# One transformer layer on one core: another fixed order of preparation and attention, the half copies of q on ScalarE, two tiles' convolution sums in PSUM, a gate's split apart from its broadcast

## The chip, the cores and the metric

The kernel runs on one core of one Trainium2 chip. The metric is the time of one execution on the device in microseconds (us). Five engines work side by side: PE (TensorE, matmuls), DVE (VectorE), ACT (ScalarE), POOL (GpSimd) and SP (which issues most of the DMAs). Each runs its own instructions in order and waits for the others through semaphores.

## The reference

One layer of a trunk with attention and a feed-forward part, for 512 latent and 128 context tokens of width 1024; 8 heads of two 64-wide sub-keys, feed-forward width 2816. Cut to what matters here:

```python
h = modulate(x, norm1_w, shift1, scale1)
proj = h @ w_in                                  # u | q | k | v | gates
q = rope_2d(q); k_lat = rope_2d(k)               # latent tokens only
s = einsum(q, concat(ctx_k, k_lat)) * scale      # two maps m = 0, 1 per head
p = softmax(s); a = p[0] - lam * p[1]
o = a @ v                                        # then RMSNorm per head
x += gate1 * ((sig(gA) * (pool(u) @ w_proj_a) + sig(gB) * (o @ w_proj_b)) @ w_out)
h = modulate(x, norm2_w, shift2, scale2)
a, up = split(h @ w_ffn_in)
a = dwconv3(a, ffn_conv_w, ffn_conv_b)           # 3 taps along the tokens
x += gate2 * ((silu(a) * up) @ w_ffn_out)        # then the final RMSNorm
```

with `rope_2d` a product with cos, plus the halves exchanged times sin. The gates, shifts and scales are rows of silu(cond) @ w_ada.

## The kernel before, in words

Tokens lie along the free dimension, channels along the partitions, 128 at a time. Each fp32 operand of a product is split in a high and a low part (`whi`, `wlo` of a weight, `hT[0]`, `hT[1]` of the activations), and each product is three matmuls: hi by hi, hi by lo, lo by hi. ACT casts the high part of a weight, DVE or POOL subtracts for the low part (`wload`, L123 to L127).

The start: norm of x, the rows of the modulation (`ada_...`), h, and the first projections of q0, k0 and q1 are written as short steps, one letter and a number each, and the string `BOOT` (L296 to L300) lists them in the order of the program. `q`, `k` and `w` are a step (six matmuls) of q0, k0 and q1 (`part`).

Attention: the string of `PHASES` (L486 to L495) gives the order, one string for each head. `p` is a projection step of six matmuls (q, k of later heads), `b` the same for v, `Sxy` the scores of token tile x under map y (`attend`: DVE takes the maximum `nm`, ACT the exponential `p` with its sum, for the second map DVE and ACT combine the two), `x` is `between` (the turns `mx` of k), `T` and `P` turn the probabilities of the head before (`pat`, `th`, `tl`) and multiply them by v. Scores share two banks of PSUM.

Ahead of a head's scores stands `rope` (L555): ACT copies the projection out of PSUM to `ry`, DVE shuffles it to `rsh`, POOL multiplies by cos, DVE by sin, DVE adds. `q_part` then makes for each map a cast `qd` (ACT), the low part `ql` (DVE) and a copy of the cast, `t[o]`, in the other 64 partitions (POOL, L584). `k_part` makes `ks` (cast on ACT, low part on DVE). Weights are loaded and split one step ahead of their use (`weights`, L793), q's and k's low part on POOL.

Instructions that are pinned keep the order in which they are written; the others are placed by the scheduler of the compiler.

Feed-forward: 22 tiles of 128 channels, in groups (`cycle`). Tiles 0 and 1 (`i < DIRECT`) form their sum of the convolution, `cv`, in SBUF, later tiles in PSUM (`conv`, `silu`): ACT writes the middle tap with the bias, DVE adds the two others to it, 511 columns for the latent and 127 for the context tokens, ACT applies silu. The second gate `g2` is worked out in steps that hang between the matmuls `acc...` of the output product (`gate2`, called at the places listed in `GATE2`, L1539): its sum is split in `bh_g` (ACT) and `bl_g` (DVE), and `pb_g`, ones times both, spreads it over the partitions (`acc_bcast`).

Of the kernel before, what the change touches and what calls it, by code (L numbers as in the profile page):

```python
# [18 lines left out]
P = 128  # L19
# [48 lines left out]
def trunk_kernel(ctx: ExitStack, tc: tile.TileContext, a: dict, o: list):  # L68
# [205 lines left out]
    def acc_bcast(acc, dst, cols, name):  # L274

        hi, lo = acc_split(acc, name)
        for c in range(2):
            pb = bank1(f"pb_{name}{c}")
            mm(pb, ones, hi[:, c, :], True, False)
            mm(pb, ones, lo[:, c, :], False, True)  # L280
            nc.scalar.copy(dst[c][:, cols], pb)
            if c == 0:
                yield
# [8 lines left out]
    with tc.tile_pool(name="boot", bufs=1, reuse_waits="tile") as boot:  # L292
# [3 lines left out]
        BOOT = ("n0 i0 n1 x0 i1 n2 x1 y0 i2 n3 x2 n4 i3 a00 y1 i4 y2 x3 a01 y3 d10 x4 d11 l10 r0 s0 l11 c0 a10 z0 u0 "  # L296
# [229 lines left out]
    with tc.tile_pool(name="att", bufs=2, reuse_waits="tile") as att:  # L526
# [28 lines left out]
        def rope(ps, name, scale):  # L555

            sh = att.tile([P, TOK], F32, tag="rsh", name=f"rsh_{name}")[:, :LAT]
            y_ = att.tile([P, TOK], F32, tag="ry", name=f"ry_{name}")
            nc.scalar.activation(two(y_), ps[:, :, :HALF], AF.Copy, scale=scale)
            y = y_[:, :LAT]  # L560
            nc.vector.stream_shuffle(sh, y, SHUF)
            nc.gpsimd.tensor_tensor(y, y, cos, ALU.mult)  # L562
            nc.vector.tensor_tensor(sh, sh, sin, ALU.mult)
            nc.vector.tensor_tensor(y, y, sh, ALU.add)
            return y_

        def q_load(h):
            return wcols(w_in, COL_Q + h * P, P, 0, KD, f"q{h}", nc.gpsimd)
# [4 lines left out]
        def q_part(h, ps=None, bank=bankP):  # L573
            if ps is None:
                w = weights("q", h)
                ps = bank(f"psq{h}")
                yield from proj_steps(ps, w, hT)
            y = rope(ps, f"q{h}", 0.125)
            qd = [att.tile([P, TOK], F32R, tag=f"qd{m}", name=f"qd{m}_{h}") for m in range(2)]
            ql = QL[h % 2]  # L580
            for (r, o, t), (_, _, l) in zip(MAPS(qd), MAPS(ql)):
                nc.scalar.copy(t[r], y[r])
                nc.vector.tensor_tensor(l[r], y[r], f(t[r]), ALU.subtract)
                nc.gpsimd.tensor_copy(t[o], f(t[r]))  # L584
            Q[h] = qd, ql
# [39 lines left out]
        def k_part(h, ps=None):  # L625
            if ps is None:
                w = weights("k", h)
                ps = bankP(f"psk{h}")
                yield from proj_steps(ps, w, hT)
            y = rope(ps, f"k{h}", 1.0)  # L630
            k_split(h, y, slice(P, KEYS))
            Y[h] = y
# [160 lines left out]
        def weights(kind, i):  # L793

            n = need.index((kind, i))
            for st in need[n:n + 2]:
                if st not in W:
# [17 lines left out]
        def step(h, op):  # L815
# [9 lines left out]
            elif kind == "P":  # L825
                values(h - 1, i)
            elif kind == "m":
# [289 lines left out]
    def conv(i):  # L1117

        av = AV.pop(i)
        cv = CVS[i] = pools["ffn"].tile([P, TOK], F32, tag="cv", name=f"cv{i}", bufs=3)  # L1120
        w = [vcol[:, V_CW + j * NF + i:V_CW + j * NF + i + 1] for j in range(3)]
        if i < DIRECT:
            SUMS[i] = cv[:, :LAT], cv[:, LAT:]
        else:
            SUMS[i] = PS[i][1], bank1(f"cvp{i}")[:, :PRO]
        segs = tuple(zip(SUMS[i], (av[:, :LAT], av[:, LAT:])))
        for c, x in segs if i >= DIRECT else ((cv, av),):
# [7 lines left out]
    def silu(i):  # L1135
        lat, pro = SUMS.pop(i)
        cv = CVS[i]
        for c, x in ((cv[:, :LAT], lat), (cv[:, LAT:], pro)) if i >= DIRECT else ((cv, cv),):
# [176 lines left out]
    def gate2():  # L1315
        for hf in range(2):
            for acc in ada_acc(ffn, 5 * D, hf, "g2", "s", "yr"):
                yield
            yield from acc_bcast(acc, g2, slice(hf * 512, hf * 512 + 512), f"g2{hf}")
# [219 lines left out]
    GATE2 = ((0, 2), (1, 0), (1, 2), (2, 0), (3, 2), (3, 4), (4, 0), (4, 2), (5, 0), (5, 2), (7, 1), (7, 3))  # L1539
# [55 lines left out]
```

## Time and profile before

| | us |
|---|---|
| median of 3 runs (1078.32 to 1081.81) | 1081.34 |
| the profiled execution | 1082.84 |
| its span, first to last instruction | 1081.1 |
| PE busy | 1038.2 (96%) |
| DVE busy | 822.4 (76%) |
| ACT busy | 549.5 (51%) |
| POOL busy | 317.5 (29%) |

The times are of the device; the profile is of one execution, whose own time stands beside its span. Busy shares are means over stages that differ: the start lasts to about 70 us, attention to about 330, the gates and merged projections to 600, output projection and second norm to 660, feed-forward to the end.

### The profile page before, as it was taken

Reading aid. Unit: us, or ns where it says so; the run is one execution under the profiler, and the core shown is the slowest. Engines: PE = TensorE matmul, PEld = TensorE weight load, DVE = VectorE, ACT = ScalarE, POOL = GpSimd, SP = SyncE. Lnnn points to the kernel's source line nnn. Section 1 sums busy time; section 2 is a strip of 40 time slices with the busy share of each in tenths; the row PEclk is TensorE's granted clock in tenths of the full one; section 3 lists DMA queues with packets and bytes.
Section 4 is the critical chain, followed back from the end, with each engine's and each line's share of the span. In section 5 each row is a group of like instructions: output and inputs, shape, how many; then the busy total and the mean of one; then the engine's idle time right before and its main releaser. Section 6 shows DMA issues by size and latency. Waiting matters only on the chain.

```text
span 1081.1 us, 16773 instructions
## 1 busy us (share of the span) xinstructions
PE 1038.2 (96%) x6559; PEld 970.1 (90%) x6559; DVE 822.4 (76%) x1193; ACT 549.5 (51%) x946; POOL 317.5 (29%) x256
## 2 busy tenths in 40 slices
PE   6997999999999999999999999999999999999997
PEld 4787899989999989999998889999779998899986
DVE  5968988988987678677773568988888874698746
ACT  8636767657676462223242465564345542165524
POOL 4444334243220650000000004462565320354211
PEclk9988999999999999999999999999999999999999
DMA  9840212112111115555555021323443322323312
GB/s 313 231 108 28 67 52 66 41 43 70 42 32 52 57 44 170 160 156 157 156 171 201 1 59 39 99 78 98 136 137 98 97 70 69 98 79 98 118 39 98
DMA packets 128481, 106.11 MB, mean 98 GB/s; under 512 B 4173, under 2 KB 110205, under 8 KB 128402
## 3 DMA queue, kind: packets, MB, share of 16 engines
q1 hardware_dynamic: 126450, 101.93, 31.0%
q0 software_dynamic: 1232, 1.80, 0.8%
q8 instruction: 51, 0.84, 0.3%
q10 hardware_dynamic: 720, 1.31, 0.3%
q14 instruction: 28, 0.23, 0.1%
HBM read 101.36 MB, written 3.67 MB: 97 GB/s over the span
## 4 chain that ended last, share of the span: by engine, by line
PE 66%; DVE 19%; ACT 6%; issue 4%; DMA 2%; POOL 1%; SPq 1%; ACTq 0%; DVEq 0%; POOLq 0%
PE ps_g L157 10%; PE psyb L157 5%; PE psk L157 3%; PE psu L157 3%; PE psya L157 3%; PE pb L157 3%; PE s L157 2%; PE po L157 2%; PE psq L157 2%; DVE nm L688 2%; PE psv L157 2%; PE acc L157 1%; PE pat L160 1%; DVE ks L599 1%; DVE p L698 1%
## 5 line engine op out<-in xcount | busy, mean ns | idle before, releaser
L150 POOL TENSOR_TENSOR s<-raw_fu 128x512 f32<-128x512 f32 x20 | 30.1, 1504 | 299.4 <-DVE spare L150 155.8
L157 PE MATMUL ps_g<-hT,whi_g 128*128 128x320 f32 x512 | 96.7, 311 | 0.0
L157 PEld LDWEIGHTS ps_g<-hT,whi_g 128*128 128x128 f32 x512 | 80.2, 188 | 2.0 <-issue 1.5
L690 ACT ACTIVATE p<-s,nm 128x640 f32<-128x640 f32 (+1 forms) x80 | 56.6, 708 | 40.0 <-DVE nm L688 39.4
L157 PE MATMUL psv<-whi_v,hT 128*128 128x256 f32 x320 | 66.3, 287 | 0.0
L688 DVE TENSOR_REDUCE nm<-s 128x1 f32<-128x640 f32 (+1 forms) x80 | 56.5, 709 | 12.4 <-PE s L157 11.0
L150 DVE TENSOR_TENSOR wlo_f<-s,whi_f 128x1024 fp32r<-128x1024 f32 x40 | 53.1, 1336 | 7.2 <-ACT whi_f L150 6.8
L157 PE MATMUL ps_g<-hT,wlo_g 128*128 128x320 f32 x256 | 58.3, 309 | 0.0
L150 ACT CAST whi_f<-s 128x1024 fp32r<-128x1024 f32 x40 | 42.3, 1058 | 27.0 <-POOL s L150 27.0
L157 PE MATMUL s<-ks,qd 128*128 128x320 f32 x144 | 44.2, 318 | 10.3 <-DVE ks L599 7.1
L157 PEld LDWEIGHTS psv<-whi_v,hT 128*128 128x128 f32 x320 | 53.5, 193 | 0.3 <-ACT whi_v L126 0.3
L150 DVE TENSOR_TENSOR wlo_f<-raw_fa,whi_f 128x1024 fp32r<-128x1024 f32 x22 | 34.5, 1567 | 21.8 <-ACT whi_f L150 21.6
L157 PE MATMUL psyb<-on,whi_pb 128*128 128x320 f32 x256 | 48.1, 310 | 0.0
L157 PE MATMUL psv<-wlo_v,hT 128*128 128x256 f32 x160 | 45.7, 285 | 0.9 <-DVE wlo_v L127 0.9
L157 PE MATMUL s<-ks,ql 128*128 128x320 f32 x144 | 43.0, 308 | 0.0
L157 PEld LDWEIGHTS ps_g<-hT,wlo_g 128*128 128x128 f32 x256 | 42.8, 188 | 0.0
L157 PE MATMUL psk<-hT,whi_k 128*128 128x320 f32 x224 | 42.6, 312 | 0.0
L157 PEld LDWEIGHTS psyb<-on,whi_pb 128*128 128x128 f32 x256 | 40.3, 188 | 0.5
L697 ACT ACTIVATE p<-p,z 128x640 f32<-128x640 f32 (+1 forms) x40 | 29.8, 744 | 20.0 <-DVE z L696 19.8
L157 PEld LDWEIGHTS s<-ks,qd 128*128 128x128 f32 x144 | 27.7, 192 | 12.9 <-POOL ry_q L562 6.8
L698 DVE SCALAR_TENSOR_TENSOR p<-p,z,p 128x640 f32<-128x640 f32 (+1 forms) x40 | 35.0, 878 | 5.4 <-ACT p L697 5.1
L157 PE MATMUL pb<-mg,whi_f 128*128 128x320 f32 x176 | 38.9, 307 | 0.0
(1046 smaller groups left out, 3437.0 us busy)
## 6 DMA issues: line engine op xcount, KB each, us to landing
raw_fa<-in_w_ffn_in_dram SPq DMA_DIRECT2D x22, 512.0 KB, 3.8
raw_fu<-in_w_ffn_in_dram SPq DMA_DIRECT2D x22, 512.0 KB, 4.0
raw_fo<-in_w_ffn_out_dram SPq DMA_DIRECT2D x20, 512.0 KB, 3.6
raw_g<-in_w_in_dram SPq DMA_DIRECT2D x16, 512.0 KB, 4.5
raw_g<-in_w_ada_dram SPq DMA_DIRECT2D x16, 512.0 KB, 3.7
araw_sh<-in_w_ada_dram SPq DMA_DIRECT2D x8, 512.0 KB, 8.4
araw_sc<-in_w_ada_dram SPq DMA_DIRECT2D x8, 512.0 KB, 8.4
raw_v<-in_w_in_dram SPq DMA_DIRECT2D x8, 512.0 KB, 6.2
```

What stands on the lines that cost most here:

```text
L150: pin(getattr(self.eng, op)(*args, **kw))
L157: pin(nc.tensor.matmul(out, s, m, start=start, stop=stop, skip_group_check=more))
L160: pin(nc.tensor.transpose(out, x, ident))
L599: nc.vector.tensor_tensor(t[o, cols], y[r], f(t[r, cols]), ALU.subtract)
L688: nc.vector.tensor_reduce(nm[:, i:i + 1], s, AX.XY, ALU.max, negate=True)
L690: nc.scalar.activation(p.rearrange("p (b n) -> p b n", b=s.shape[1]), s, AF.Exp, bias=nm[:, i:i + 1], accum_out=z[:, i:i + 1])
L697: nc.scalar.activation(p, p, AF.Copy, scale=z[:, 1:2])
L698: nc.vector.scalar_tensor_tensor(A[h, t], A[h, t], z[:, 0:1], p, ALU.mult, ALU.add)
```

## The change

It writes another order in `BOOT` and `PHASES` (the same steps, with one new step `w` in phase 0), takes the cos product of q0, q1 and k0 from POOL to DVE, the half copies of q from POOL to ACT, makes q2's weights ready at the step `w` with DVE and ACT, puts the sums of tiles 0 and 1 in PSUM like the others, and lets a step pass between the split and the broadcast of the second gate. The first string of `PHASES` stands for all.

```diff
-        "3b p 4b 2p 2b S00 S01 2b p S10 2p x p S11 p b S20 2b S21 b S30 3b S31 S40 2b",
-        "3p S00 p S01 2p x 2p T0 S10 4p S11 T1 p P0 p S20 2p S21 P1 T2 2p P2 p S30 p S31 2p S40 2p",
+        "b p b 2p 7b S00 b S01 x w b p S10 2p S11 b p S20 p b S21 4b S30 2b S31 S40 b",
+        "2p S00 2p S01 p x 3p T0 S10 4p S11 T1 p P0 p S20 2p S21 T2 P1 2p P2 p S30 2p S31 p S40 2p",
...
-        def rope(ps, name, scale):
+        def rope(ps, name, scale, eng=nc.gpsimd):
...
-            nc.gpsimd.tensor_tensor(y, y, cos, ALU.mult)
+            eng.tensor_tensor(y, y, cos, ALU.mult)
...
-        def q_load(h):
-            return wcols(w_in, COL_Q + h * P, P, 0, KD, f"q{h}", nc.gpsimd)
+        def q_load(h, *eng):
+            return wcols(w_in, COL_Q + h * P, P, 0, KD, f"q{h}", *(eng or (nc.gpsimd,)))
...
-            y = rope(ps, f"q{h}", 0.125)
+            y = rope(ps, f"q{h}", 0.125, nc.gpsimd if h > 1 else nc.vector)
...
-                nc.gpsimd.tensor_copy(t[o], f(t[r]))
+                nc.scalar.copy(t[o], f(t[r]))
...
-            y = rope(ps, f"k{h}", 1.0)
+            y = rope(ps, f"k{h}", 1.0, nc.gpsimd if h > 0 else nc.vector)
...
-                if st not in W:
+                if st not in W and (st, kind) != (("q", 2), "v"):
...
+            elif kind == "w":
+                W["q", 2] = q_load(2, dve, act)
...
-        if i < DIRECT:
-            SUMS[i] = cv[:, :LAT], cv[:, LAT:]
-        else:
-            SUMS[i] = PS[i][1], bank1(f"cvp{i}")[:, :PRO]
+        SUMS[i] = PS[i][i >= DIRECT], bank1(f"cvp{i}")[:, :PRO]
...
-        for c, x in segs if i >= DIRECT else ((cv, av),):
+        for c, x in segs:
...
-    def acc_bcast(acc, dst, cols, name):
+    def acc_bcast(acc, dst, cols, name, apart=False):
...
         hi, lo = acc_split(acc, name)
+        if apart:
+            yield
...
-            yield from acc_bcast(acc, g2, slice(hf * 512, hf * 512 + 512), f"g2{hf}")
+            yield from acc_bcast(acc, g2, slice(hf * 512, hf * 512 + 512), f"g2{hf}", True)
...
-    GATE2 = ((0, 2), (1, 0), (1, 2), (2, 0), (3, 2), (3, 4), (4, 0), (4, 2), (5, 0), (5, 2), (7, 1), (7, 3))
+    GATE2 = ((0, 2), (1, 0), (1, 2), (2, 0), (3, 1), (3, 2), (3, 4), (4, 0), (4, 2), (5, 0),
+             (5, 2), (7, 0), (7, 2), (7, 3))
```

How it moves instructions shows at three places. The first is DVE behind the split of the second v weight (`wlo_v01`), up to the low parts of the first keys (`ks0_0` and `ks1_0`, the two maps of head 0), ahead of the first scores; before:

```order
L561 STREAM_SHUFFLE rsh_q0_750<-ry_q0_751 128x512
L561 STREAM_SHUFFLE rsh_k0_765<-ry_k0_766 128x512
L563 TENSOR_TENSOR rsh_q0_750<-rsh_q0_750,sin_707 128x512
L563 TENSOR_TENSOR rsh_k0_765<-rsh_k0_765,sin_707 128x512
L564 TENSOR_TENSOR ry_q0_751<-ry_q0_751,rsh_q0_750 128x512
L583 TENSOR_TENSOR ql00_708<-ry_q0_751,qd0_0_757 64x640
L583 TENSOR_TENSOR ql01_709<-ry_q0_751,qd1_0_758 64x640
L564 TENSOR_TENSOR ry_k0_766<-ry_k0_766,rsh_k0_765 128x512
L561 STREAM_SHUFFLE rsh_q1_776<-ry_q1_777 128x512
L563 TENSOR_TENSOR rsh_q1_776<-rsh_q1_776,sin_707 128x512
L599 TENSOR_TENSOR ks0_0_742<-ry_k0_766,ks0_0_742 64x640
L599 TENSOR_TENSOR ks1_0_743<-ry_k0_766,ks1_0_743 64x640
```

and now:

```order
L563 STREAM_SHUFFLE rsh_q0_750<-ry_q0_751 128x512
L563 STREAM_SHUFFLE rsh_k0_765<-ry_k0_766 128x512
L564 TENSOR_TENSOR ry_q0_751<-ry_q0_751,cos_706 128x512
L565 TENSOR_TENSOR rsh_q0_750<-rsh_q0_750,sin_707 128x512
L564 TENSOR_TENSOR ry_k0_766<-ry_k0_766,cos_706 128x512
L565 TENSOR_TENSOR rsh_k0_765<-rsh_k0_765,sin_707 128x512
L566 TENSOR_TENSOR ry_q0_751<-ry_q0_751,rsh_q0_750 128x512
L566 TENSOR_TENSOR ry_k0_766<-ry_k0_766,rsh_k0_765 128x512
L585 TENSOR_TENSOR ql00_708<-ry_q0_751,qd0_0_757 64x640
L585 TENSOR_TENSOR ql01_709<-ry_q0_751,qd1_0_758 64x640
L601 TENSOR_TENSOR ks0_0_742<-ry_k0_766,ks0_0_742 64x640
L601 TENSOR_TENSOR ks1_0_743<-ry_k0_766,ks1_0_743 64x640
```

The cos products of q0 and k0 have joined DVE's row, the add of k0 stands ahead of the low parts `ql`, and the shuffle and sin product of q1 have left the place ahead of the keys. On ACT at the same place, before:

```order
L126 CAST whi_v01_803<-raw_v01_801 128x1024
L559 ACTIVATE ry_q0_751<-psq0_372 128x640
L559 ACTIVATE ry_k0_766<-psk0_361 128x640
L126 CAST whi_q2_809<-raw_q2_807 128x1024
L582 CAST qd0_0_757<-ry_q0_751 64x640
L582 CAST qd1_0_758<-ry_q0_751 64x640
L559 ACTIVATE ry_q1_777<-psq1_429 128x640
L598 CAST ks0_0_742<-ry_k0_766 64x640
L598 CAST ks1_0_743<-ry_k0_766 64x640
```

and now:

```order
L126 CAST whi_v01_803<-raw_v01_801 128x1024
L561 ACTIVATE ry_q0_751<-psq0_394 128x640
L561 ACTIVATE ry_k0_766<-psk0_362 128x640
L584 CAST qd0_0_757<-ry_q0_751 64x640
L584 CAST qd1_0_758<-ry_q0_751 64x640
L600 CAST ks0_0_742<-ry_k0_766 64x640
L600 CAST ks1_0_743<-ry_k0_766 64x640
L586 CAST qd0_0_757<-qd0_0_757 64x640
L586 CAST qd1_0_758<-qd1_0_758 64x640
L561 ACTIVATE ry_q1_777<-psq1_429 128x640
```

The cast of q2's weight (`whi_q2`) has left, the half copies (`qd` from `qd`) stand behind the casts of the keys, and the copy of q1 out of PSUM behind them. The second place is PE where q0's projection (`psq0`) ends, here its last row with what follows up to the key projection of head 1 (`psk1`); before:

```order
L157 MATMUL psq0_372<-hT0_98,wlo_first1_514 128x320 x2
L157 MATMUL psq1_429<-hT0_98,whi_first2_369 128x320 x2
L157 MATMUL psq1_429<-hT1_99,whi_first2_369 128x320 x2
L157 MATMUL psq1_429<-hT0_98,wlo_first2_370 128x320 x2
L157 MATMUL psv00_823<-whi_v01_803,hT0_98 128x256
L157 MATMUL psv00_823<-wlo_v01_804,hT0_98 128x256
L157 MATMUL psv00_823<-whi_v01_803,hT1_99 128x256
L157 MATMUL psv00_823<-whi_v01_803,hT0_98 128x256
L157 MATMUL psv00_823<-wlo_v01_804,hT0_98 128x256
L157 MATMUL psv00_823<-whi_v01_803,hT1_99 128x256
L157 MATMUL psk1_842<-hT0_98,whi_k1_718 128x320 x2
```

and now:

```order
L157 MATMUL psq0_394<-hT0_98,wlo_first1_505 128x320 x2
L157 MATMUL psq1_429<-hT0_98,whi_first2_372 128x320 x2
L157 MATMUL psq1_429<-hT1_99,whi_first2_372 128x320 x2
L157 MATMUL psq1_429<-hT0_98,wlo_first2_373 128x320 x2
L157 MATMUL psq1_429<-hT0_98,whi_first2_372 128x320 x2
L157 MATMUL psq1_429<-hT1_99,whi_first2_372 128x320 x2
L157 MATMUL psq1_429<-hT0_98,wlo_first2_373 128x320 x2
L157 MATMUL psk1_824<-hT0_98,whi_k1_718 128x320 x2
```

The step of q1 (`psq1`) and v (`psv01`) that came ahead now come behind: in both programs 182 rows stand ahead of the first scores. The third place is PE at the second half of the second gate, in the output product (`acc...`); before:

```order
L157 MATMUL acc010C_7950<-wlo_fo016_8073,g00_7016 128x512
L157 MATMUL acc010C_7950<-whi_fo016_8072,g01_7017 128x512
L157 MATMUL pb_g210_8130<-bh_g21_8126,ones_85 128x512
L157 MATMUL pb_g210_8130<-bl_g21_8127,ones_85 128x512
L157 MATMUL acc014_7953<-whi_fo016_8072,g00_7016 128x512
L157 MATMUL acc014_7953<-wlo_fo016_8073,g00_7016 128x512
```

and now:

```order
L157 MATMUL acc010C_7956<-wlo_fo016_8079,g00_7022 128x512
L157 MATMUL acc010C_7956<-whi_fo016_8078,g01_7023 128x512
L157 MATMUL acc014_7959<-whi_fo016_8078,g00_7022 128x512
L157 MATMUL acc014_7959<-wlo_fo016_8079,g00_7022 128x512
L157 MATMUL acc014_7959<-whi_fo016_8078,g01_7023 128x512
L157 MATMUL acc014_7959<-whi_fo016_8078,g00_7022 128x512
L157 MATMUL acc014_7959<-wlo_fo016_8079,g00_7022 128x512
L157 MATMUL acc014_7959<-whi_fo016_8078,g01_7023 128x512
L157 MATMUL pb_g210_8142<-bh_g21_8126,ones_85 128x512
L157 MATMUL pb_g210_8142<-bl_g21_8127,ones_85 128x512
```

The broadcast pair `pb_g` of the gate has moved behind one tile of six matmuls.

## Rows read from the trace of the kernel before

**Rows 1.** The page, part 1: busy us (share), instructions

```profile
PE 1038.2 (96%) x6559; PEld 970.1 (90%) x6559; DVE 822.4 (76%) x1193; ACT 549.5 (51%) x946; POOL 317.5 (29%) x256
```

**Rows 2.** PE's waits: line waited for, total us, times, longest us

```profile
PE s L157 <- DVE ks L599: 7.1, 2, 6.6
...
PE mx L160 <- ACT p L690: 3.3, 3, 1.4
...
PE pb_g L157 <- DVE bl_g L250: 1.9, 2, 1.4
...
PE pf2A L157 <- ACT av L150: 1.4, 1, 1.4
...
PE s L157 <- DVE tl L714: 1.3, 1, 1.3
```

**Rows 3.** Windows: length, busy us by engine, granted clock, DMA share, GB/s

```profile
86.00:91.00 5.00, 4.61 (x21) 4.64 (x22) 4.29 (x8) 2.12 (x5) 0.00 (x0) 0.55 0.00 0
108.00:135.00 27.00, 24.99 (x163) 23.15 (x162) 24.65 (x37) 19.89 (x39) 8.83 (x7) 1.00 0.22 67
```

**Rows 4.** Timeline of PE, 69 to 87 us: start, duration, [idle before]

```profile
69.39 0.46 PE L157 MATMUL psq<-hT,wlo_first 128*128 128x320 f32 x2
...
74.89 0.40 PE L157 MATMUL psv<-whi_v,hT 128*128 128x256 f32 x2
...
75.61 0.40 PE L157 MATMUL psv<-whi_v,hT 128*128 128x256 f32 x2
...
76.45 0.75 PE L157 MATMUL psk<-hT,whi_k 128*128 128x320 f32 x4
...
77.33 0.75 PE L157 MATMUL psk<-hT,whi_k 128*128 128x320 f32 x4
...
86.39 0.61 PE L157 MATMUL s<-ks,qd 128*128 128x320 f32 x1 [6.58 <-DVE ks L599]
```

**Rows 5.** The timeline of the other engines, 69 to 84 us

```profile
69.64 1.05 ACT L126 CAST whi_v<-raw_v 128x1024 fp32r<-128x1024 f32 x1 [0.59 <-issue]
...
70.71 0.70 ACT L559 ACTIVATE ry_q<-psq 128x640 f32<-128x640 f32 x1
70.72 1.23 DVE L127 TENSOR_TENSOR wlo_v<-raw_v,whi_v 128x1024 fp32r<-128x1024 f32 x1 [1.26 <-ACT whi_v L126]
...
71.87 0.74 DVE L561 STREAM_SHUFFLE rsh_q<-ry_q 128x512 f32<-128x512 f32 x1
...
73.93 2.85 POOL L127 TENSOR_TENSOR wlo_q<-raw_q,whi_q 128x1024 fp32r<-128x1024 f32 x1
...
74.45 2.89 DVE L563 TENSOR_TENSOR rsh_k<-rsh_k,sin 128x512 f32<-128x512 f32 x1
...
76.75 1.74 POOL L562 TENSOR_TENSOR ry_k<-ry_k,cos 128x512 f32<-128x512 f32 x1
...
77.26 1.78 DVE L564 TENSOR_TENSOR ry_q<-ry_q,rsh_q 128x512 f32<-128x512 f32 x1
...
83.75 0.69 DVE L563 TENSOR_TENSOR rsh_q<-rsh_q,sin 128x512 f32<-128x512 f32 x1
```

**Rows 6.** The tile qd: ns of one, min/median/max, first and last start

```profile
L582 ACT CAST qd<-ry_q x16: 710/725/732, 79.1 to 293.3; 64x640 fp32r<-64x640 f32 x16
...
L584 POOL CAST qd<-qd x16: 712/1202/1829, 80.0 to 295.3; 64x640 fp32r<-64x640 f32 x16
```

**Rows 7.** The tiles cv and pf2C, DVE's convolution sums

```profile
L150 DVE SCALAR_TENSOR_TENSOR cv<-spare,vcol,cv x8: 338/1526/1789, 662.5 to 679.7; 128x511 f32<-128x511 f32 x4, 128x127 f32<-128x127 f32 x4
...
L150 DVE SCALAR_TENSOR_TENSOR pf2C<-av,vcol,pf2C x2: 754/754/755, 686.0 to 686.8; 128x511 f32<-128x511 f32 x2
```

**Rows 8.** The timeline of DVE and ACT, 675 to 681 us

```profile
675.91 4.13 DVE L150 SCALAR_TENSOR_TENSOR cv<-spare,vcol,cv 128x511 f32<-128x511 f32 x4
...
680.13 0.74 ACT L150 ACTIVATE cv<-cv 128x640 f32<-128x640 f32 x1 [4.41 <-DVE cv L150]
```

**Rows 9.** The timeline of DVE at the gate, 797 us

```profile
797.68 2.19 DVE L250 TENSOR_TENSOR bl_g<-acc_g,bh_g 128x1024 fp32r<-128x1024 f32 x1
```

More of the change, by code (lines that the diff above doesn't have):

```diff
@@ L295, in trunk_kernel @@
         H_POOL = (7,)
-        BOOT = ("n0 i0 n1 x0 i1 n2 x1 y0 i2 n3 x2 n4 i3 a00 y1 i4 y2 x3 a01 y3 d10 x4 d11 l10 r0 s0 l11 c0 a10 z0 u0 "
[4 rows of a table removed]
+        BOOT = ("n0 n1 i0 x0 i1 n2 x1 i2 a00 y0 n4 n3 i3 x2 y2 i4 x3 a01 y3 d10 x4 y1 d11 l10 r0 s0 l11 c0 a10 z0 u0 "
[4 rows of a table added]
         pinned[0] = True
@@ L1119, in conv @@
         av = AV.pop(i)
-        cv = CVS[i] = pools["ffn"].tile([P, TOK], F32, tag="cv", name=f"cv{i}", bufs=3)
+        CVS[i] = pools["ffn"].tile([P, TOK], F32, tag="cv", name=f"cv{i}", bufs=3)
         w = [vcol[:, V_CW + j * NF + i:V_CW + j * NF + i + 1] for j in range(3)]
-        if i < DIRECT:
-            SUMS[i] = cv[:, :LAT], cv[:, LAT:]
-        else:
-            SUMS[i] = PS[i][1], bank1(f"cvp{i}")[:, :PRO]
+        SUMS[i] = PS[i][i >= DIRECT], bank1(f"cvp{i}")[:, :PRO]
         segs = tuple(zip(SUMS[i], (av[:, :LAT], av[:, LAT:])))
-        for c, x in segs if i >= DIRECT else ((cv, av),):
+        for c, x in segs:
             act.activation(c, x, AF.Identity, bias=vcol[:, V_CB + i:V_CB + i + 1], scale=w[1])
@@ L1137, in silu @@
         cv = CVS[i]
-        for c, x in ((cv[:, :LAT], lat), (cv[:, LAT:], pro)) if i >= DIRECT else ((cv, cv),):
+        for c, x in ((cv[:, :LAT], lat), (cv[:, LAT:], pro)):
             act.activation(c, x, AF.Silu)
```

22 rows, old and new, of tables (BOOT, PHASES) are left out of this document.

## The prediction

> **What bounds the kernel now.** I read the page first: PE is busy 1038.2 of 1081.1 us, DVE 822.4, ACT 549.5, POOL 317.5 [rows 1]. PE sets the end, so a change is worth what it takes from PE's waits, from the time PE spends at its lower clock, or from its work; the change removes and adds no matmul. PE stands still for about 43 us. The view of PE's waits says for whom: the one long wait is 6.6 us for the split keys `ks`, then 3.3 us in three waits of the key turns `mx` for exponentials, 1.9 us for `bl_g`, 1.4 us of `pf2A` for the copy `av`, 1.3 us for `tl` [rows 2]. [...]
>
> **The long wait, step by step.** PE starts the first scores at 86.39, after 6.58 us without work [rows 4]. What it waits for starts when q0's projection ends, its last matmuls at 69.39 for 0.46, so 69.85; call it T. The rows behind T [rows 5]: ACT first casts `whi_v`, 1.05, then copies q and k out of PSUM, 0.70 each. DVE splits `wlo_v`, 1.23, and shuffles, 0.74. POOL does the cos product of q, then takes q2's weight split, 2.85, which stands ahead of the cos product of k, 1.74 from 76.75. Meanwhile the sin product of k on DVE takes 2.89 and the add of q 1.78, where the same form takes 0.69 with POOL idle. So the chain is stretched by POOL twice: by its queue and by running beside DVE.
>
> The new order does three things here. (1) Of the same 182 rows of PE that come ahead of the first scores, one step of q1 (six matmuls, 0.88, the distance of the `psk` rows) and one v step (six, 0.72, the distance of the `psv` rows) now come behind q0's end [rows 4]. T moves to 69.85 - 0.88 - 0.72 = 68.25, and PE keeps 2 q1 steps, 3 k1 steps and 8 v steps for the time behind T: 1.76 + 2.64 + 5.76 = 10.16 us. (2) The cos products of q0, q1 and k0 go to DVE, and q2's split leaves its place between them, so POOL has nothing there. (3) The half copies of q go to ACT, behind the casts of `ks`.
>
> The new chain from T, with durations of undisturbed rows [rows 5]: ACT `whi_v` 1.05; DVE `wlo_v` 1.23, to T + 2.3 (q and k are copied out by T + 2.5). Then two shuffles of 0.74 and five ops of 0.69 (cos and sin of q and of k, add of q), 4.9 end to end, some 0.6 less as successive DVE ops start before the former's end: add q is done at T + 6.6 to 7.2. Then five casts on ACT of 0.73 (two of q, two of `ks`, the first half copy) [rows 6], 3.65: the first scores start at T + 10.25 to 10.95 with a handover, 78.5 to 79.2. PE's own cover lasts to 78.4, so a wait of 0.1 to 0.8 stands where 6.6 stood. **Term 1: -7.4 us** (86.39 to 79.0). Ends: -5.9 if a DVE or ACT row of the chain is stretched once as the 2.89 was, -8.7 if the six q0 matmuls that now come earlier also fill an idle stretch ahead of 53 us.
>
> **The rest of phase 0.** In the window at 0.55 PE is 4.61 us busy [rows 3]; at full clock that is 2.5, so 2.1 are won if the low clock does not come back. Against it: the new phase has fewer projection steps between the first scores and the key turn `x`, so `x` and the scores around it wait longer for exponentials, and q2's split now takes 1.23 of DVE and 1.05 of ACT inside the phase. I cost that as one more wait like the longest of `mx`, 1.4 [rows 2], less a little: an estimate. **Term 2: -0.8** (0 to -2.0).
>
> **The rest of attention.** For it: the casts leave POOL, where the 16 took 1.2 us each in the median beside DVE's work; they cost 16 x 0.73 = 11.7 us of ACT instead [rows 6]. Phases 3, 5 and 7 begin with scores at once, so the exponential that `mx` waits for (3.3 us in three waits) starts one to three steps of 0.88 earlier. Against it: ACT has about 26% room in its full stretches [rows 3], and each pair of copies pushes what follows by 1.46. What PE can still win here is bounded by rows 2, some 4.6 us from the `mx` and `tl` rows and a few small waits. **Term 3: -1.0** (-4 to +3): a third of the 3.3 us, the copies paying the rest back.
>
> **Convolution of the first two tiles.** In SBUF the eight DVE ops, four of 511 columns and four of 127, have a median of 1526 ns and go up to 1789; the same op with its sum in PSUM took 754 [rows 7]. So the four ops of conv 1 take DVE at most 3.0 us (if the short ones took as long as the long ones), an estimated 2.2, instead of 4.13 [rows 8], conv 0 the like; ACT pays four more short instructions. Who waits: `silu` of conv 1 ended an idle time of 4.41 on ACT for DVE, `av` was queued behind it, and `pf2A` on PE behind `av`, 1.4 [rows 2, 8]. With `silu` 2 us earlier that wait goes. **Term 4: -1.5** (0 to -2.7, DVE's two relieved stretches helping a later tile too). [...]
>
> **The gate row.** `bl_g` starts at 797.68 and takes 2.19, and PE waits 1.4 for it [rows 2, 9]. Behind it stand six independent matmuls of `acc`, 512 columns wide where those of a `psk` step of 0.88 are 320, so 1.4 us, and the new order puts just these ahead of the broadcast pair. The copy of the gate behind it comes no later than now, since PE reaches it no later. **Term 5: -1.2** (0 to -1.4).
>
> At nothing I cost: the start up to T (the same 143 steps; its waits for `hT` and `araw` may move either way by about 1), the exchanged loads of k3 and the cached keys (both needed a phase later), and the three cos products' 2.1 us on DVE in the boot, covered by PE's 10.16.
>
> **Sum.** -7.4 - 0.8 - 1.0 - 1.5 - 1.2 = -11.9. The profiled execution took 1082.84, 1.74 beyond its span and 1.5 above the median 1081.34: it would come to 1070.9 with a span near 1069.2, and the median to about 1069.4.
>
> **Rivals.**
> *The attention waits close too.* The kernel wins most of term 3's room: PE's `mx` and `tl` waits (4.6) go, and the longer end of terms 1 and 2: 1069.4 - 3.0 - 1.3 - 1.2 = about 1064. For it: POOL's traffic leaves DVE, which was stretched in several rows. Against: DVE is 91% busy there and gets three products and a split more.
> [...]
> *ACT takes POOL's place.* If each pair of half copies delays PE once (exponentials queued behind it hold one of the two score banks), 8 x 1.46 = 11.7 us eat the gain: 1081, no change. If it is met twice for a head, at the exponentials behind it and at the next head's scores, which now come sooner and read the copies, 23.4: 1092.8, slower. It decides from 1.5 us per head on. Against it: ACT's 26% of room is 8.6 us in a head's 33, and the copies are made some steps ahead of their scores.
> *The moved phases do nothing beyond the start*, and terms 3 to 5 fall to zero because another wait ends last at each place: 1081.34 - 8.2 = 1073.
>
> **How the numbers follow.** Chances: the forecast 0.42, with its own range 1066.5 to 1072; the closing waits (below 1066.5) 0.20; the smaller win (the second and the fourth rival, 1072 to 1078) 0.27; ACT without change 0.07; ACT slower 0.04. From 1063 to 1076.5 all but about 2 in 10 is held. No change is within 0.3%, 3.2 us, about what a measurement of this kernel can tell: faster 0.89, same 0.07, slower 0.04.
>
> **What would show it.** Right: the first scores within 1 us of the `psv` step ahead of them, at 78 to 80 us; no stretch with a granted clock of 0.55 behind it; the add of q at 0.7 instead of 1.78; no wait of `pf2A` for `av` and none of `pb_g` over 0.3; ACT's busy time up by about 12 us, POOL's down by some 25. Wrong: a wait of several us for `ks` or `qd` at the first scores; waits of `s` for ACT's `qd` in every head; a new wait in the gate's or FFN's first tiles; or a boot that ends q0 later than 68.5.

## The result and the profile after

The changed kernel takes 1071.78 us (median of 4 runs, 1070.32 to 1072.72) against 1081.05 for the kernel before measured beside it (1078.32 to 1081.81): a ratio of 0.9918, 95% interval 0.9900 to 0.9937, so 8.9 us less (6.8 to 10.8). The forecast was 1069.4. The profiled execution is the fastest of the four, with a span of 1068.5, and the one of before was the slowest of its series (1082.84), so the two spans differ by 12.6 us where the medians differ by 9.3. The stretches below are read from these two profiles and add up to 12.6 us, some 3.7 more than the change is worth; part of that is the clock, as will be seen.

The page of the changed kernel, parts 1 and 2:

```profile
PE 1032.8 (97%) x6559; PEld 965.0 (90%) x6559; DVE 810.9 (76%) x1197; ACT 561.8 (53%) x966; POOL 294.6 (28%) x236
...
PEclk9999999999999999999999999999999999999999
```

ACT has the 12 us more, POOL 23 less that 16 copies, three products and a split make [rows 1]. PE's own busy time fell by 5.4 us with the same 6559 matmuls while the mean granted clock rose from 0.990 to 0.997, by 0.007 of the span or some 7 us: time at a lower clock for the most part, an estimate from these two. Now what PE waits for (line, what, total, times, longest):

```profile
PE pat L160 <- ACT p L692: 3.4, 2, 2.1
...
PE s L157 <- DVE ks L601: 2.3, 2, 1.8
...
PE pf8C L157 <- DVE wlo_f L150: 1.9, 1, 1.9
...
PE s L157 <- ACT p L692: 1.8, 2, 1.2
...
PE pf5A L157 <- ACT av L150: 1.1, 1, 1.1
...
PE mx L160 <- ACT p L692: 0.5, 1, 0.5
```

Against [rows 2]: the 6.6 us for `ks` are gone (the 1.8 left belong to head 1), `mx` fell from 3.3 to 0.5, the waits of `pb_g` for `bl_g` and of `pf2A` for `av` are no longer among the waits; but `pat` and `pf8C`, which waited 1.5 and 0.5 before, wait 3.4 and 1.9. Those two before:

```profile
PE pat L160 <- ACT p L690: 1.5, 1, 1.5
...
PE pf8C L157 <- DVE wlo_f L150: 0.5, 1, 0.5
```

Behind the long wait and up to the end of attention PE's waits sum to 8.6 us before and to 8.5 now: in attention they have moved, not shrunk. The place of the long wait on PE's timeline:

```profile
66.40 0.46 PE L157 MATMUL psq<-hT,wlo_first 128*128 128x320 f32 x2
...
77.45 0.28 PE L157 MATMUL psv<-whi_v,hT 128*128 128x256 f32 x1
77.57 0.31 PE L157 MATMUL s<-ks,qd 128*128 128x320 f32 x1
```

The first scores follow a v step without any idle time, at 77.57 instead of 86.39 [rows 4]. The chain that fed them, on the other engines:

```profile
66.65 1.05 ACT L126 CAST whi_v<-raw_v 128x1024 fp32r<-128x1024 f32 x1 [1.24 <-issue]
...
67.73 1.23 DVE L127 TENSOR_TENSOR wlo_v<-raw_v,whi_v 128x1024 fp32r<-128x1024 f32 x1 [1.94 <-ACT whi_v L126]
...
70.15 0.68 DVE L564 TENSOR_TENSOR ry_q<-ry_q,cos 128x512 f32<-128x512 f32 x1
...
71.95 0.69 DVE L565 TENSOR_TENSOR rsh_k<-rsh_k,sin 128x512 f32<-128x512 f32 x1
72.55 0.68 DVE L566 TENSOR_TENSOR ry_q<-ry_q,rsh_q 128x512 f32<-128x512 f32 x1
...
76.31 1.48 ACT L586 CAST qd<-qd 64x640 fp32r<-64x640 f32 x2
```

The sin product of k, 2.89 in [rows 5], takes 0.69, the add of q 0.68 instead of 1.78, with no work on POOL from 62.8 to 81.2 us. The 0.69 in [rows 5] was not one with POOL idle: POOL's cos product of q1 started 0.11 us behind it, at 83.86, and took 1.70, so not every row beside POOL is stretched. q0's projection ends at 66.86 (the T of the prediction: 66.40 and 0.46), and the first scores stand 10.71 us behind it, where 10.25 to 10.95 was worked out; before it was 16.54. T itself came 3.0 us earlier than before, not 1.6. The windows that answer to [rows 3]:

```profile
86.00:91.00 5.00, 4.91 (x34) 4.47 (x34) 4.53 (x8) 4.90 (x9) 0.29 (x1) 1.00 0.35 105
108.00:135.00 27.00, 26.46 (x178) 25.14 (x177) 23.61 (x41) 20.64 (x38) 4.46 (x4) 1.00 0.19 58
```

No low clock follows, 1.00 where 0.55 stood, and between 108 and 135 us PE is busy for 1.5 us more. In the feed-forward part the convolution sums of tile 0 take 748 to 755 ns in PSUM (answer to [rows 7]), and `bl_g` takes 2.20 as before [rows 9], at 785.26, but its wait has moved:

```profile
L150 DVE SCALAR_TENSOR_TENSOR pf0A<-spare,vcol,pf0A x2: 748/752/755, 651.5 to 652.3; 128x511 f32<-128x511 f32 x2
```

```profile
800.38 0.41 PE L157 MATMUL pf8C<-mg,wlo_f 128*128 128x320 f32 x1 [1.90 <-DVE wlo_f L150]
802.90 0.42 PE L157 MATMUL pf9A<-mg,wlo_f 128*128 128x320 f32 x1 [0.49 <-DVE wlo_f L150]
```

By stretches, from the times at which PE starts the same work in both profiles (the end of attention is the first `psu`, here now and then before):

```profile
307.61 0.75 PE L157 MATMUL psu<-hT,whi_u 128*128 128x320 f32 x4
```

```profile
318.33 0.75 PE L157 MATMUL psu<-hT,whi_u 128*128 128x320 f32 x4
```

The gains and losses: to the first scores 8.8 us won; from there to the first scores of head 1 0.2 lost (24.4 to 24.6); from there to the first `psu`, the end of attention, 2.1 won (207.5 to 205.4); from there to the end 1.9.

### The profile page after: what moved, and what is told of

Same layout as the page of the kernel before. It is cut to its first block, busy times and chain, and to the rows that moved or that the text cites. A ratio compares the mean times of both kernels' runs of the same rounds, so it can differ in the third digit from the quotient of the medians.

```text
span 1068.5 us, 16757 instructions
## 1 busy us (share of the span) xinstructions
PE 1032.8 (97%) x6559; PEld 965.0 (90%) x6559; DVE 810.9 (76%) x1197; ACT 561.8 (53%) x966; POOL 294.6 (28%) x236
## 4 chain that ended last, share of the span: by engine, by line
PE 74%; DVE 12%; ACT 5%; issue 3%; POOL 2%; DMA 2%; SPq 0%; ACTq 0%; POOLq 0%; DVEq 0%
PE ps_g L157 11%; PE psyb L157 5%; PE psk L157 4%; PE psu L157 3%; PE acc L157 3%; PE psya L157 3%; PE pb L157 3%; PE psv L157 3%; PE s L157 2%; PE psq L157 2%; PE po L157 2%; POOL s L150 2%; PE pat L160 1%; DVE nm L690 1%; DMA raw_fu<-in_w_ffn_in_dram 1%
## 5 line engine op out<-in xcount | busy, mean ns | idle before, releaser
L690 DVE TENSOR_REDUCE nm<-s 128x1 f32<-128x640 f32 (+1 forms) x80 | 56.7, 710 | 12.4 <-PE s L157 10.6
L126 ACT CAST whi_g<-raw_g 128x1024 fp32r<-128x1024 f32 x16 | 16.8, 1050 | 40.5 <-PE ps_g L157 21.8
```

The source lines that it names most:

```text
L126: cp.copy(hi[:, :n], rv)
L690: nc.vector.tensor_reduce(nm[:, i:i + 1], s, AX.XY, ALU.max, negate=True)
```

## The experiments

Each kernel was timed against the kernel before on one chip; the ratios compare with 0.9918 for the changed kernel, 0.001 being 1.08 us. The intervals are 1.3 to 3 us wide on either side, that of the changed kernel itself 2, so what is smaller is read from the trace.

**e1, the old start order.** `BOOT` as before, the rest as changed.

> The changed kernel with the old order of the start (BOOT) and all else kept. Theory (the cover behind q0 is what holds PE): q0 ends one q1 step and one v step later, 1.6 us, and only 8.6 us of work lie behind it where the chain of whi_v, rope and splits takes 10.9, so the first scores wait 2 to 2.5 us for ks or qd; time 1073.5 to 1076 against 1071.8. Rival (the order of the start is worth nothing, the gain came from POOL leaving the chain): no wait over 0.5 us at the first scores and a time within 1 us of 1071.8.

Measured: 1070.29, 0.9904 (0.9875 to 0.9932), no slower. The theory falls: the first scores come at 78.37 with no wait. q0's projection ends at 67.50, 2.35 us earlier than before although `BOOT` is the same, and the strings of phase 0 supply the cover; what is left of the order of `BOOT` is another wait, 1.49 us of `psk` for the bank that the copy of k empties, 0.46 in the changed kernel:

```profile
69.87 0.57 PE L157 MATMUL psk<-hT,whi_k 128*128 128x320 f32 x2 [1.49 <-ACT ry_k L561]
```

Up to 76 us the mean granted clock is 0.93 in the three profiles with the old order and 0.96 or 0.98 in those with the new one, whose waits ahead of the first scores are longer instead (14 to 15 us against 13): the two about cancel.

**e2, three cos products back on POOL.**

```diff
-            y = rope(ps, f"q{h}", 0.125, nc.gpsimd if h > 1 else nc.vector)
+            y = rope(ps, f"q{h}", 0.125)
-            y = rope(ps, f"k{h}", 1.0, nc.gpsimd if h > 0 else nc.vector)
+            y = rope(ps, f"k{h}", 1.0)
```

> The changed kernel with the cos products of q0, q1 and k0 back on POOL, q2's weight split left at the step w. Theory (POOL's queue was the price, not the product itself): with nothing ahead of them the two cos products run beside DVE's sin products, the add of k comes 0 to 1 us later, the first scores wait 0 to 1 us, time +0.5 (0 to +1.5). Rival (running beside POOL is the price): a sin product and an add on DVE stretch to 1.4 to 2.9 us each as before, the first scores wait 3 us, time +3.

Measured: 1075.34, 0.9959 (0.9938 to 0.9979), 4.4 us slower than the changed kernel. Each theory has a half. The first scores come at 77.30 after a wait of 0.16, as the first has it; the sin products do stretch, to 1.38 and 1.78, but inside PE's cover. The price is paid behind: q1's chain on DVE now stands ahead of the first maximum `nm`, which starts at 81.02 instead of 78.36, and `mx` waits:

```profile
82.81 0.33 PE L160 MATMUL mx<-ident,ry_k 128*128 128x128 f32 x1 [3.40 <-ACT p L692]
```

All of the price lies in phase 0: from the first scores to those of head 1 it takes 29.1 us, 24.6 in the changed kernel. The scheduler moved 14 rows of DVE with this edit, so the price is not that of POOL alone.

**e3, q2's split back on POOL at the first v step, no step `w`.**

```diff
-                if st not in W and (st, kind) != (("q", 2), "v"):
+                if st not in W:
```

> The changed kernel with q2's weight load and split back at the first v step, low part on POOL, and no step w; the cos products stay on DVE. Theory of the queue: no product of the chain stands behind the split any more, so only one or two DVE rows beside it stretch, 1 to 2 us, the first scores wait about 1 to 1.5 us, and phase 0 gets back 1.2 us of DVE: time 0 to +1. Rival (running beside POOL is the price): 2.4 to 2.9 us of POOL stop DVE for as long, the first scores wait 2.5 us or more and the time is +2.5 to +4 with the low clock behind it.

Measured: 1073.95, 0.9938 (0.9916 to 0.9961). The first scores wait 1.5 us for the half copy of `qd` and attention behind them takes 231.0 us from first scores to `psu` (230.0 in the changed kernel): the queue theory by the trace, its +0 to +1 and the measured +2.2 not told apart.

**e4, the half copies back on POOL.**

```diff
-                nc.scalar.copy(t[o], f(t[r]))
+                nc.gpsimd.tensor_copy(t[o], f(t[r]))
```

> The changed kernel with the 16 half copies of q back on POOL (1.2 us each there) instead of ACT (0.73). Theory: ACT's 11.7 us lie in its idle time and POOL's copies stretch the low parts ql beside them, by 0.3 us each and more, so the time goes up by 1 (0 to +2) and the attention ends 1 us later. Rival (ACT has become a bound in attention, with pat and s waiting 5 us for its exponentials): the copies leave ACT's path and the time falls by 1 to 3 us.

Measured: 1077.44, 0.9976 (0.9960 to 0.9992): 6.3 us slower, three times the most that the theory allowed, and the rival has the wrong sign, with these strings of `PHASES` (e5 and e9 compare the copies with the old ones). From the first scores to `psu` attention takes 236.2 instead of 230.0. DVE's low parts `ql`, in e4 and then in the changed kernel (count, busy us, mean ns):

```profile
L585 DVE TENSOR_TENSOR ql<-ry_q,qd 64x640 fp32r<-64x640 f32 x16 | 16.7, 1045 | 1.1 <-ACT qd L584 0.7
```

```profile
L585 DVE TENSOR_TENSOR ql<-ry_q,qd 64x640 fp32r<-64x640 f32 x16 | 13.1, 817 | 0.6 <-ACT qd L584 0.2
```

That is 3.6 us of DVE in attention, where it is the busiest engine but PE (208.3 of 242 us from 78 to 320, ACT 164.2). PE's waits there grow from 8.5 to 12.7 us, spread over `s`, `mx` and `pat`, and the granted clock, 1.00 all through attention in the changed kernel, is 0.91 from 200 to 220 and from 240 to 260 us. Here too rows moved, more than 20 on DVE.

**e5, the old strings of `PHASES`,** with `w` put behind the `x` of phase 0.

> The changed kernel with the old strings of PHASES (the step w put behind x of phase 0), start, engines, convolution and gate as changed. Theory: between the first scores and the end of attention the new strings are worth about 2 us, so the time is +1 to +3 and the waits of mx for exponentials of phases 1, 3 and 5, 3.3 us in the kernel before, are back. Rival: the strings only move the waits (from mx to pat), time within 0.7 us.

Measured: 1080.71, 1.0008 (0.9994 to 1.0022): as slow as the kernel before, with everything else changed. The first scores stand at 80.46, 5.9 us earlier than before, and `psu` at 317.61 against 318.33: what was won ahead of them is lost behind. That is three times the most that the theory allowed, and the rival fails too. Two thirds of the loss lie in phase 0, which takes 29.5 us from the first scores to those of head 1 instead of 24.6:

```profile
80.46 0.41 PE L157 MATMUL s<-ks,qd 128*128 128x320 f32 x1 [0.28 <-ACT qd L586]
...
110.00 0.30 PE L157 MATMUL s<-ks,qd 128*128 128x320 f32 x1
```

From there to `psu` it is 207.6 against 205.4, the 2 us that the theory had for the strings. PE's waits by total, times and longest:

```profile
PE s L157 <- ACT p L692: 4.9, 5, 1.9
...
PE mx L160 <- ACT p L692: 2.3, 2, 1.5
PE s L157 <- DVE tl L716: 2.0, 1, 2.0
```

**e6, the old gate.**

```diff
-            yield from acc_bcast(acc, g2, slice(hf * 512, hf * 512 + 512), f"g2{hf}", True)
+            yield from acc_bcast(acc, g2, slice(hf * 512, hf * 512 + 512), f"g2{hf}")
```

and the old `GATE2`.

> The changed kernel with the gate's broadcast right behind its split again (old GATE2, no extra step). Theory (the gain is given back at the next wait for DVE): PE waits 1.4 us for bl_g again, but pf8C then waits 0.5 instead of 1.9, since the DVE row that it needs comes at the same time; time within 0.5 us of the changed kernel. Rival (the prediction's term): +1.2 to +1.4.

Measured: 1070.77, 0.9920 (0.9896 to 0.9944), no change. The trace shows the two waits side by side:

```profile
787.73 0.50 PE L157 MATMUL pb_g<-bl_g,ones 128*128 128x512 f32 x1 [1.42 <-DVE bl_g L250]
...
800.62 0.41 PE L157 MATMUL pf8C<-mg,wlo_f 128*128 128x320 f32 x1 [0.54 <-DVE wlo_f L150]
```

1.42 + 0.54 with the old gate, 1.90 with the new one: the row of DVE that `pf8C` needs comes when it came.

**e7, the old convolution** (sums of tiles 0 and 1 in `cv`, as in the diff ahead).

> The changed kernel with the convolution sums of tiles 0 and 1 back in SBUF. Theory: the DVE ops take 1.5 to 1.8 us beside POOL's sums again, silu of tile 1 comes 2 us later, pf2A waits 1.3 us for av; time +1.4. [...]

Measured: 1073.05, 0.9939 (0.9914 to 0.9964), +2.3 with intervals that overlap. By the trace `pf2A` waits 0.93 us for `av` again, and 23.0 us pass from `pf2A` to `pf4A`, 21.9 in the changed kernel. At `pf5A` the changed kernel waits 1.1 us, e7 none and e6, which has the new convolution, none either: that wait comes and goes.

**e8, the split of the third sum earlier,** at the first tile of the second and third group.

```diff
         sums(i, 1)
+        hilo(i, 3)
         hilo(i, 4)
...
-        elif i == first:
-            hilo(i, 3)
```

> The changed kernel with one split brought forward: at the first tile of the second and third group of the feed-forward part the split of the third weight sum stands in the preparation, ahead of the last additions of the group before on DVE, instead of behind the first products. Theory (DVE's queue from bl_g on ends last at pf8C): the wait of 1.9 us of pf8C for wlo_f goes, time -1 to -1.9. Rival (the load of the next tile's weights ends last): pf9A waits instead, time within 0.5 us.

Measured: 1075.52, 0.9960 (0.9946 to 0.9974), 4.5 us slower. The wait of `pf8C` goes, and `pf9A` waits 3.49 where it waited 0.49, with a granted clock of 0.74 from 798 to 811 us. DVE in that stretch:

```profile
797.22 1.79 DVE L1418 TENSOR_TENSOR x<-x,yr 128x512 f32<-128x512 f32 x1
798.93 1.78 DVE L150 TENSOR_TENSOR ul<-raw_fu,uh 128x512 fp32r<-128x512 f32 x1
800.64 0.68 DVE L1417 TENSOR_TENSOR yr<-acc011C,g 128x512 f32<-128x512 f32 x1
801.35 1.05 DVE L1418 TENSOR_TENSOR x<-x,yr 128x512 f32<-128x512 f32 x1
802.33 0.47 DVE L150 TENSOR_TENSOR av<-av,pb 128x320 f32<-128x320 f32 x1
802.73 1.89 DVE L150 TENSOR_TENSOR wlo_f<-raw_fa,whi_f 128x1024 fp32r<-128x1024 f32 x1
```

It works without a pause; another order only chooses who waits for it, and rows put off met POOL's sums, which run from 796.57 on with gaps under 0.1 us (`ul` takes 1.78 us, 0.68 in the changed kernel).

**e9, the start alone.** The kernel before with the new `BOOT`, the three cos products on DVE and q2's split at `w`; old strings, copies on POOL, old convolution and gate.

> The kernel before with the start alone changed: the new BOOT, the cos products of q0, q1 and k0 on DVE, q2's split at a step w behind x of phase 0; old strings of PHASES, half copies on POOL, old convolution and gate. Theory (a package: what PE wins ahead of the first scores is given back in phase 0, where DVE and ACT are the bound): first scores at 78 to 81 us as in the changed kernel, against 86.4 before, but the second head's first scores win 3 us or less; the time is 1 to 4 us under that of the kernel before. Rival (the prediction's sum: each term stands for itself): 8 us under it.

Measured: 1076.41, 0.9968 (0.9955 to 0.9981), 3.5 us under the kernel before. The time is in the range of the theory, its reason is not: the first scores come at 79.49, 6.9 us earlier than before, those of head 1 still 5.5 earlier, where the theory had 3 or less, and `psu` 5.8. So little of what is won ahead of the first scores is given back in this trace. The two spans differ by 6.6 us, the medians by 3.5: the profile of the kernel before is of an execution 2.7 us above the median of its runs beside e9. In phase 0 a wait that the kernel before had as 0.93 is longer:

```profile
79.49 0.38 PE L157 MATMUL s<-ks,qd 128*128 128x320 f32 x1 [0.74 <-DVE ks L599]
89.68 0.63 PE L157 MATMUL s<-ks,qd 128*128 128x320 f32 x1 [2.73 <-ACT p L690]
...
105.26 0.31 PE L157 MATMUL s<-ks,qd 128*128 128x320 f32 x1
...
312.50 0.75 PE L157 MATMUL psu<-hT,whi_u 128*128 128x320 f32 x4
```

e5 has the same start and strings with the copies on ACT, and the new convolution and gate. It is 4.3 us slower than e9, with intervals that do not overlap, and phase 0 takes 29.5 us in it, 25.8 here. So with the old strings the copies on ACT cost time, with the new ones they win it (e4); and with the copies on POOL the new strings win nothing (e4 against e9: 0.9 us slower, with intervals that overlap).

**e10, all but the start:** old `BOOT`, cos and q2's split on POOL, the rest as changed.

> The changed kernel with the old start: old BOOT, all cos products on POOL, q2's split on POOL from the first v step, no step w; new strings of PHASES, half copies on ACT, convolution and gate as changed. Theory (package): the first scores stand at 85 to 87 us after a wait of 5 us or more, and attention behind them takes as long as in the changed kernel or up to 3 us less, since DVE has less to do in phase 0: time +4 to +7 over the changed kernel's 1071.8. Rival (the prediction's sum): +8 or more, the whole of term 1 and 2.

Measured: 1079.28, 0.9989 (0.9973 to 1.0004), 7.7 us slower than the changed kernel and not told apart from the one before; between the bounds of the two expectations. The wait is back, but it is 3.72 us and not 5 or more: q0's projection ends at 67.46, 2.4 us earlier than before, and the first scores stand 14.73 us behind it, 16.54 before. And attention behind them takes 234.9 us, where the expectation had the 230.0 of the changed kernel or less: phase 0 alone takes 28.5, with a granted clock of 0.75 from 82.2 to 89 us and a wait of 2.37 for `mx`.

```profile
82.19 0.42 PE L157 MATMUL s<-ks,qd 128*128 128x320 f32 x1 [3.72 <-DVE ks L601]
```

**e11, projection steps moved to the waits that are left.**

```diff
-        "2p S00 2p S01 p x 3p T0 S10 4p
+        "4p S00 p S01 p x 2p T0 S10 4p
...
-        "S00 4b S01 x 2p T0 2p S10 b p b P0
+        "S00 4b S01 x 3p T0 p S10 b p b P0
-        "S00 p S01 4p x T0 3p S10 P0 S11 p T1 2p S20 3p T2 2p S21 P1 P2 p S30 S31 4p S40 3p",
+        "S00 p S01 4p x 2p T0 2p S10 P0 S11 p T1 2p S20 3p T2 2p S21 P1 P2 p S30 S31 3p S40 3p",
```

> The changed kernel with three strings of PHASES moved by a few projection steps: phase 1 takes two more ahead of its first scores (which wait 1.75 us for ks), phases 4 and 5 one and two more ahead of the first turns T0 (which wait 1.3 and 2.1 us for an exponential). Theory (PE runs ahead of ACT at these places and has work that can stand there): the three waits, 5.1 us, fall under 2 in sum, the time is -1.5 to -4 against the changed kernel. Rival (DVE and ACT are the bound through these phases, so PE waits at the next place instead): waits of attention stay at 8 us in sum, time within 1 us.

Measured: 1081.27, 1.0008 (0.9996 to 1.0020), 9.7 us slower. The three waits fell from 5.1 to 0.8 us, as meant, and others came, 14.3 us in sum: 2.1 of `mx` and 1.4 of `pat` in phases 1 and 2, and the longest where the steps moved had ended a projection sooner and the next one found its PSUM bank not yet emptied by ACT:

```profile
253.84 1.44 PE L157 MATMUL psk<-hT,whi_k 128*128 128x320 f32 x4 [3.46 <-ACT ry_q L561]
```

**e12, all 16 cos products on DVE.**

> The changed kernel with all cos products on DVE, the 13 of the later heads too; all else kept. In the changed kernel these 13 take 1.3 to 1.8 us each on POOL, and the sin products on DVE beside them 1.0 to 1.24 in the mean instead of 0.69. Theory (what POOL reads beside DVE costs DVE as long as it takes, as in the rerun with three products back on POOL): the sin products fall to 0.69, 6 us of DVE come back for 8 us of products, the key and query chains of each head get shorter by about 0.6 us, time -1 to -3. Rival (DVE, 85% busy and more through attention, is the bound, and 13 x 0.6 = 8 us more on it are not paid back): time +1 to +4, the waits of PE in attention rise from 8.5 us.

Measured: 1079.54, 0.9994 (0.9980 to 1.0009), 8.2 us slower. The theory's first half is seen: the sin products of q fall from 1237 to 685 ns in the mean. Its second is not: PE's waits in attention go from 8.5 to 11.9 us, most of them for exponentials:

```profile
PE s L157 <- ACT p L692: 5.2, 5, 2.1
...
PE pat L160 <- ACT p L692: 4.0, 3, 1.6
```

That it is the 8 us of products is not shown: DVE's busy time from the first scores to `psu` is 197.0 us, 198.7 in the changed kernel, so the rows that no longer run beside POOL paid the products back in sum. Nearly 60 other rows of DVE have moved with it, and what remains is where rows stand; which of them costs the time was not told apart.

No version tried beats the changed kernel; e1 and e6 equal it within what can be measured, and e3 and e7 come out 2 us slower with intervals that overlap its own.

## Why the forecast held, and where its steps did not

**Term 1 (-7.4): right, in chain and size; the origin of T was not.** The first scores moved by 8.8 us in the profile: T by 3.0 and the chain behind it by 5.8, forecast 1.6 and about 5.8. Seven profiles with this start (the changed kernel, e4, e6, e7, e8, e11, e12) have the first scores between 76.98 and 80.89, all without a wait, and in each they stand 10.70 or 10.71 us behind the end of q0. What differs is T, 66.27 to 70.18 with a median of 68.5, where 68.25 was forecast; the median of the first scores, 79.2, is 7.2 us earlier than before, so the 8.8 holds some luck of the execution. What POOL costs in the chain shows apart from T: 10.7 us without its products and its split, 11.0 with the cos products back (e2), 12.4 with q2's split back (e3), 14.7 with both (e10). The step that T moves by 1.6 us through the order of the start, and that this supplies the cover, failed in part: with the old `BOOT` and the new strings T is 67.5 (e1, e10), no later than with the new one.

**Term 2 (-0.8): the sign failed.** The low clock behind the wait is gone, 1.00 from 86 to 91 us for 0.55, which I keep at the estimated 2.1 from [rows 3]: before, the score matmuls start 0.27 us apart from 86.79 to 88.39, at a clock of 0.50, and 0.15 apart from 91.81 to 92.25, at 1.00. But the waits from there to head 1's first scores grew from 1.3 us (two of `s` for exponentials) to 3.5 (0.55 of `mx`, 1.21 of `s` for an exponential, 1.75 of head 1's `ks`), by 2.2 and not by the 1.3 that I had allowed: 0.2 lost.

**Term 3 (-1.0): 2.1 in the profile, and costed in the wrong way.** I treated the new strings as something to win a third of `mx`'s waits with and the copies as paying part of that back. e5 and e4 show that the kernel needs both: without the new strings it is 9.7 us slower, without the copies on ACT 6.3. And each needs the other: of the four pairings with the new start, old strings with copies on POOL (e9) or ACT (e5), new strings with copies on POOL (e4) or ACT (the changed kernel), e5 is 4.3 us slower than e9, e4 no faster, and only the last gains, 5.4 us with its convolution.

**Term 4 (-1.5): 1.4 by `pf4A`,** the mechanism as told, by the trace alone, since e7's time does not settle it: sums in PSUM at 0.75 us, no wait of `pf2A` (0.93 in e7). These sums had POOL at work beside them too, two sums of 2.35 and 2.43 us, and were not stretched: 0.75 in PSUM stands against up to 1.79 in SBUF beside POOL. The short sums, 338 ns at the least in SBUF [rows 7], take 348 to 355 in PSUM, some 10 ns more.

```profile
L150 DVE SCALAR_TENSOR_TENSOR cvp<-spare,vcol,cvp x4: 348/353/355, 652.9 to 666.9; 128x127 f32<-128x127 f32 x4
```

A later wait for `av` hides part of it in some executions.

**Term 5 (-1.2): nothing.** The step that failed is "the copy of the gate comes no later, so the wait is won": I followed PE past the pair, not DVE. DVE's queue from `bl_g` on was unaltered: from its start to that of `pf8C` behind its wait 15.1 us pass in both profiles, and PE met it 13 us later at `pf8C`. e6 shows it, and e8 that DVE is full there. One longer wait also stands where two shorter ones stood: in the nine profiles in which `pf8C` waits 1.9 us, the granted clock from 795 to 815 us is 0.91 in five, 1.00 in four; in the three with the old gate (before, e6, e9) it is 1.00. The changed kernel, then e1:

```profile
795.00:815.00 20.00, 17.61 (x119) 17.09 (x119) 18.85 (x21) 9.72 (x16) 13.10 (x8) 1.00 0.28 80
```

```profile
795.00:815.00 20.00, 18.11 (x114) 17.85 (x113) 18.05 (x21) 9.50 (x16) 12.03 (x8) 0.91 0.35 102
```

**The sum.** The terms were added as if each stood for itself. The start alone is worth 3.5 us (e9), all the rest alone 1.2 (e10), both together 8.9: about 4 us, 1 to 7 by the intervals, belong to neither. The traces show where: from the first scores to those of head 1 it takes 24.4 us before and 24.6 in the changed kernel, 25.8 in e9 and 25.9 in e4, but 28.5 in e10, 29.1 in e2 and 29.5 in e5. The three long ones have the half copies on ACT together with the cos products on POOL or the old string of phase 0, and PE's long waits in them are for exponentials of ACT. Why just these pairs cost 4 to 5 us there stays open. I had put DVE's 91% share (24.65 of 27 us [rows 3]) in front of the rival of closing waits only; as a limit on term 1 it was not among the rivals. The forecast of 11.9 less lies 3 us beyond the measured 8.9; that it was no further off owes something to luck, with term 3 half its size in the profile, term 2 of the wrong sign and term 5 nothing.

The rivals: *ACT takes POOL's place* is refuted by e4 for the strings as changed, but with the old ones it holds in part (e5 against e9). A long wait that shrinks and does not go, the second rival of the chances, is what e10 looks like: 3.72 us of it are left, with a granted clock of 0.75 behind it, from 82.2 to 89 us. *The attention waits close too* did not come about, they are 8.5 us. *The moved phases do nothing beyond the start* is refuted by e5 and e9: the start alone wins 3.5 us and not 8.2.

## What to carry to other kernels

Where an engine beside PE is nearly full, as DVE was here with 7.97 of 8 us from 798 to 806, a wait taken away in one place can come back whole at the next one, as 1.4 us did from the gate to `pf8C`: follow the engine that was waited for, not PE, until a place where it has idle time, and only then count the gain. An order written out by hand belongs to the durations it was written for: here each single part put back or pushed on in attention cost 2 to 10 us, so the parts of such a change can't be costed one by one, and alone-and-undone pairs (e9 and e10) measure what they have in common. Which engine should take small copies is a question of that order too: in the new one ACT's 11.6 us (16 of 0.727) were free and POOL's slowed DVE by 3.6 us in `ql`, in the old one the same copies on ACT cost 4.3 us.

## What the runs showed of the hardware

The granted clock is not the same from one execution to the next, behind the same wait. PE waits 2.0 to 2.1 us for an exponential at the second `pat` that waits, in nine of the profiles; from 240 to 262 us the granted clock is 0.92 in six of them and 1.00 in three. The changed kernel and e6 have the same program there:

```profile
240.00:262.00 22.00, 19.56 (x134) 18.36 (x133) 18.63 (x27) 14.50 (x26) 4.44 (x4) 1.00 0.28 81
```

```profile
240.00:262.00 22.00, 19.92 (x129) 19.25 (x128) 18.69 (x27) 13.86 (x25) 5.84 (x5) 0.92 0.27 81
```

Right behind the wait, from 246 to 251 us, the granted clock is 1.00 in the changed kernel and 0.66 in e6. So this wait of 2 us costs its own length and, in some executions, nearly as much again in matmuls at a lower clock: an estimated 1.8 us, 0.08 of 22. The four runs of the changed kernel lie in two pairs as well: spans of 1068.5 and 1069.1 us with a mean clock of 0.997 and 0.996, and twice 1070.9 with 0.994 and 0.993. Only the first was profiled, so at which wait the other pair lost its clock is not known; a profile of one execution can be off the median through this by an estimated 2 us, from the 1.8 to 2.4 between the pairs.
